# Attention's wide pairs with five PSUM banks, decay vectors in another place, sigmoids behind a copy, five raw weight slots

## The chip, the cores and the metric

One core of one Trainium2 chip runs the whole decoder layer. The metric is the device time of one execution in microseconds. TensorE multiplies (PE; PEld is its weight load), VectorE (DVE) and ScalarE (ACT) do the elementwise work, GpSimd (POOL) mostly issues transfers here, and SyncE (SP) issues the loads of weights. Each engine runs its own instructions strictly in order and waits on semaphores for the others.

## The reference, cut to what matters

```
f = swiglu(rms_norm(h, ffn1_norm_pre), ffn1_w_gate, ffn1_w_up, ffn1_w_down)
h = h + 0.5 * rms_norm(f, ffn1_norm_post)

u = rms_norm(h, mix_norm_pre)
q, k, v, xr, yr, gl = jnp.split(u @ w_in, splits, axis=-1)
# three groups of four heads, dilated windows, softmax over each window,
# the three groups merged by their log-sum-exp
attn_d = attn.reshape(B, S, ATTN_OUT_WIDTH) @ w_attn_branch

log_a = -LRU_C * gate_a * jax.nn.softplus(-a_param)
a = jnp.exp(log_a); b = jnp.sqrt(-jnp.expm1(2.0 * log_a)) * (gate_x * xc)
_, hs = lax.associative_scan(combine, (a, b), axis=1)
rec_d = (hs * jax.nn.gelu(yr)) @ w_rec_branch

gates = jax.nn.sigmoid(gl).reshape(B, S, N_BRANCHES, D_MODEL)
merged = gates[:, :, 0] * attn_d + gates[:, :, 1] * rec_d
h = h + rms_norm(merged @ w_out, mix_norm_post)
# and a second swiglu block of the form of the first
```

512 positions, 1024 wide, 12 heads of 128, feed-forward width 2816, all in float32. The only part of it that is not a matmul and that the change moves is `softplus(-a_param)`, 1024 values in all, and `sigmoid(gl)` for the first of the two branches.

## The kernel before, in words

**Numbers.** A float32 operand is held as two parts that TensorE takes at its fast rate: a high part, which is a copy by ACT (L302), and the rest, a subtraction by DVE (L303). Of each product of two operands three matmuls are done (high by high, high by low, low by high), at L315 to L317 for plain products. So each weight tile of 128x1024 that arrives as `raw` costs one ACT and one DVE instruction before TensorE can use it (`split`, L299 to L303).

**Weights.** One stream of weights, `in_w`, is read in a fixed order by SP (L242) into tiles `raw` of 128x1024 float32 that rotate through four slots; a load is issued when the slot's former tile has been read for the last time. The split tiles `w8` and `w4` have four and two slots of their own.

**Products by seven.** The large products are done in blocks of 2x2 with seven products in place of eight (p1 to p7); the sums of weight quarters that this needs are made by DVE (L691 to L696, L713; in the values stage L1221). The feed-forward blocks use `seven`'s narrow form for gate and up (L729 to L731) and `down7` for the way back (L1035 to L1037, which write banks `aux`; ACT seeds and empties these at L1024 and L1040).

**Wide pairs.** Queries, keys and the sigmoid inputs come from `seven_wide`: a product is four matmuls of 512 columns (L779: high weights by both parts of the activations) and four of 256 (L780: low weights by the high part) in turn, and its two outputs lie side by side in one bank. Seven products follow one another: p1, p5, p6, p2, p7, p3, p4. Between them a partial sum is kept in PSUM: `move` (L784) has ACT copy a whole bank into another, so that the next product accumulates on top of it; `fold` (L790, L791) has ACT copy one half out and DVE add the other; `sum_of` (L797, L798) has DVE add to sums that were folded out before. Four of the five `acc` banks serve a pair. The third move copies p7's sum into the bank of p1 and p2, `b`, once `fold(b, g[0])` has read it, since p4 has to accumulate on the copy.

**Order of the stages.** Feed-forward 1, the norms of boundary 1, the values (L1193 to L1195 `values_first`, L1236 to L1238 `values_two`), then for each of four heads three groups' queries and keys (`qk`, twelve wide pairs) with attention's own small work (`attend`) written between them: scores L1340 and L1341, exponentials L1359 and L1375, an exchange of maxima between partitions L1383 to L1389, transposes L1412, the weighted values L1430 and L1435. Then four wide pairs 52 to 59 whose outputs g and u go through a sigmoid (L1449, L1450), attention's output product, the recurrent part (LRU), its output product, boundary 2, and feed-forward 2. The decay vectors `po` and `sp8` (softplus of the recurrence's parameter, as a polynomial in 128x8 tiles) are made at the start of the LRU part (L1484 to L1500), 28 tiny DVE instructions and one exponential on ACT (L1486). They are first read as scales in the LRU's gates, at L1607.

**What sets the order.** A scheduler orders the instructions of each engine by the order of the source and by priorities: `high_priority(offset=...)` pulls its block forward (EVAC 200 for what empties banks, AHEAD 100 for weights), so that code of a later place in the source can come out among earlier code where its operands allow it. `issue_after(x)` only holds a block back until x has been placed. A function of ACT that is not in its loaded table needs a table load ahead of it (rows ACT_TABLE_LOAD).

**Space.** `npool` holds two 128x512 tiles, `acc` and `r`, for the norm at the start; `first_t` holds the first 512 columns of weights beside the small parameters `sm`. Both live for the whole kernel.

Of the kernel before, what the change touches and what calls it, by code (L numbers as in the profile page):

```python
# [10 lines left out]
F32 = mybir.dt.float32  # L11
F32R = mybir.dt.float32r
AF = mybir.ActivationFunctionType
ALU = mybir.AluOpType
AX = mybir.AxisListType

P = 128
T = 512
# [11 lines left out]
EPS = 1e-6  # L30
HB = 256
RAW_W = 1024
NEG = -1.0e30

FIRST_ON = {1: 5, 2: 5}
# [138 lines left out]
SMALL = {}  # L174
# [4 lines left out]
SMALL_W = _o  # L179
# [4 lines left out]
def hybrid_layer(ctx: ExitStack, tc: tile.TileContext, xT: bass.AP, xN: bass.AP, wst: bass.AP,  # L184
                 first: bass.AP, rows: bass.AP, consts: bass.AP, bias: bass.AP, out: bass.AP):
    nc = tc.nc
    DVE, ACT, PE = nc.vector, nc.scalar, nc.tensor

    cpool = ctx.enter_context(tc.tile_pool(name="cpool", bufs=1))
    bpool = ctx.enter_context(tc.tile_pool(name="bpool", bufs=6))  # L190
    wpool = ctx.enter_context(tc.tile_pool(name="wpool", bufs=4))
    tpool = ctx.enter_context(tc.tile_pool(name="tpool", bufs=4))
    npool = ctx.enter_context(tc.tile_pool(name="npool", bufs=1))
    psum = ctx.enter_context(tc.tile_pool(name="psum", bufs=1, space=bass.MemoryType.PSUM))
    dpool = ctx.enter_context(tc.tile_pool(name="dpool", bufs=1, space=bass.MemoryType.DRAM))

    first_t = cpool.tile([P, 512 + SMALL_W], F32, name="first")
    sm = first_t[:, 512:]
    cst = cpool.tile([P, CONST_W], F32, name="cst")
    ones = cpool.tile([P, P], F32, name="ones")  # L200
    eps = cpool.tile([P, 1], F32, name="eps")
    facc = cpool.tile([P, KC, T], F32, name="facc")
# [31 lines left out]
    def raw_of(key, dst=None):  # L234

        g, i = state["g"], state["i"]
        grp = groups[g]
        if i == 0:
            w = grp[-1][1] + grp[-1][2]
            raw = dst if dst is not None else wpool.tile([P, RAW_W], F32, name="raw", tag="raw", bufs=4)  # L240
            src = bass.AP(tensor=wst.tensor, offset=wst.offset + state["off"], ap=[[w, P], [1, w]])
            nc.sync.dma_start(raw[:, :w], src)  # L242
            state["raw"] = raw
            state["off"] += w * P
        k, o, w = grp[i]
        assert k == key, (k, key)
        src = state["raw"][:, o:o + w]
        if i + 1 == len(grp):
            state["g"], state["i"] = g + 1, 0
        else:  # L250
            state["i"] = i + 1
        return src
# [23 lines left out]

    def fetch_start():

        raws = [wpool.tile([P, RAW_W], F32, name="raw", tag="raw", bufs=4) for _ in range(4)]
        wts = []  # L280
        for k in range(KC):
            raw = raws[k // 2][:, (k % 2) * 512:(k % 2) * 512 + 512]
            if k == 0:
                raw = first_t[:, :512]
                nc.sync.dma_start(hm(k), xT[k])
                nc.sync.dma_start(raw, first[:, :512])
            else:
                nc.sync.dma_start(raw, bass.AP(tensor=wst.tensor, offset=wst.offset + (k - 1) * 512 * P,
                                               ap=[[512, P], [1, 512]]))
                nc.sync.dma_start(hm(k), xT[k])  # L290
            if k % 2 == 0:
                wt = w8()
            o = (k % 2) * 512
            wts.append((wt[:, 0, o:o + 512], wt[:, 1, o:o + 512], raw))
        state["g"], state["off"] = KC, (KC - 1) * 512 * P
        return wts
# [8 lines left out]
    def acc_ps():  # L305
        return psum.tile([P, T], F32, name="acc", tag="acc", bufs=5)
# [45 lines left out]
    HALVES = (slice(0, HB), slice(HB, T))  # L352
# [406 lines left out]
        seventh(t, w, "p4", v, False)  # L759
        u0(v)  # L760

    def seven_wide(t, w, g, u, seen=lambda ap: ap):


        b, v, z, y = (acc_ps() for _ in range(4))

        def two(ps):
            return ps[:, :HB], ps[:, HB:]

        def product(p, ps, start):  # L770
            at = t[p].at
            part, cross = ps.rearrange("q (s c) -> q s c", s=2), two(ps)[1]
            if len(at(0, 0).shape) == 3:
                part = ps.rearrange("q (s b t) -> q s b t", s=2, b=2)
                cross = cross.rearrange("q (b t) -> q b t", b=2)
            for k in range(4):
                ks = slice(k * P, (k + 1) * P)
                wh, wl = w[p][:, 0, ks], w[p][:, 1, ks]
                PE.matmul(part, wh, at(BOTH, k), start=start and k == 0, stop=False, skip_group_check=True)  # L779
                PE.matmul(cross, wl, at(0, k), start=False, stop=k == 3, skip_group_check=True)  # L780

        def move(dst, src):
            with tc.high_priority(offset=EVAC):
                ACT.activation(dst, src, AF.Copy)  # L784

        def fold(ps, dst=None):
            out = tpool.tile([P, HB], F32, name="c", tag="c", bufs=CB) if dst is None else dst
            x, y_ = two(ps) if dst is None else map(seen, two(ps))
            with tc.high_priority(offset=EVAC):
                ACT.activation(out, x, AF.Copy)  # L790
                DVE.tensor_add(out, y_, out)  # L791
            return out

        def sum_of(dst, ps, c):
            x, y_ = two(ps)
            with tc.high_priority(offset=EVAC):
                DVE.tensor_add(c, x, c)  # L797
                DVE.tensor_add(dst, seen(y_), seen(c))  # L798

        product("p1", b, True)  # L800
        move(y, b)
        product("p5", z, True)
        c5 = fold(z)
        product("p6", y, False)
        move(v, y)
        c6 = fold(y)
        product("p2", b, False)
        fold(b, g[0])
        product("p7", v, False)
        move(b, v)  # L810
        sum_of(u[1], v, c5)
        product("p3", z, False)
        sum_of(g[1], z, c6)
        product("p4", b, False)
        fold(b, u[0])

    def seven(t, w, z, g, u):

# [284 lines left out]
    ap1 = ff1.enter_context(tc.tile_pool(name="act1", bufs=1))  # L1103
    new_h()
    u1 = act_of(*act_two(ap1))
    acc = npool.tile([P, T], F32, name="acc", tag="acc", bufs=1)
    nc.scalar.dma_start(sm, first[:, 512:])
    warm(eps)

# [2 lines left out]
        PE.matmul(wu[:, :P], ones, ones, start=True, stop=True)  # L1112
    wts = fetch_start()
    pss = [acc_ps() for _ in range(4)]
    r1 = npool.tile([P, T], F32, name="r", tag="r", bufs=1)
    for k in range(KC):
        wh, wl, raw = wts[k]
        if k == 0:

            z = hm(0)  # L1120
            ACT.activation(u1.hi[0], z, AF.Copy, scale=col("g1a", 0))
            for sl in HALVES:
                tail = ACT.activation(wh[:, sl], raw[:, sl], AF.Copy).ins
            DVE.scalar_tensor_tensor(u1.lo[0], z, col("g1a", 0), u1.hi[0].bitcast(F32),
                                     op0=ALU.mult, op1=ALU.subtract)
# [35 lines left out]
    kpool = kpool_cm.__enter__()  # L1161

    def rec_half():

        return kpool.tile([P, 8, T], F32R, name="rb", tag="rb")

    with ExitStack() as mx:
        tpl = mx.enter_context(tc.tile_pool(name="attn_out", bufs=1))
# [37 lines left out]
        def values_two(steps, then):  # L1206
# [76 lines left out]
            for j in range(2):  # L1283
# [4 lines left out]
        t, steps = forms_of(lambda i, j: Form(lambda s, k: um_t[2 * i + k // 2][:, s, k % 2, HALVES[j]]),  # L1288
                            apool, False, rec_half)
# [12 lines left out]
        def pair_of(key):  # L1302

            i = order.index(key)
            if i + 1 < len(order):
                forms[order[i + 1]] = w_forms(order[i + 1])
            return forms.pop(key)
# [131 lines left out]

        for hd in range(NH):  # L1440
            attend(hd, qkvs.pop(hd))
            if hd + 1 < NH:
                qkvs[hd + 1] = qk(hd + 1)


        for c in range(0, KC, 2):
            g, u = tmp("g"), tmp("u")
            seven_wide(t, pair_of(("pair", 52 + c, 53 + c)), [g[:, h] for h in HALVES], [u[:, h] for h in HALVES])
            ACT.activation(facc[:, c, :], g, AF.Sigmoid)  # L1449
            ACT.activation(facc[:, c + 1, :], u, AF.Sigmoid, scale=-1.0)  # L1450
        apool_cm.__exit__(None, None, None)
        for c in range(KC):
            ps = acc_ps()
# [5 lines left out]
    with ExitStack() as mx:  # L1459
# [15 lines left out]
        lpool = lpool_cm.__enter__()  # L1475


        def s8(name):
            return lpool.tile([P, 8], F32, name=name)
        o, w = SMALL["ap"]  # L1480
        av = sm[:, o:o + w]
        na, ex, zz, po = (s8(n) for n in ("na", "ex", "zz", "po"))
        sp8 = s8("sp8")
        DVE.tensor_scalar(na, av, -1.0, None, op0=ALU.mult)  # L1484
        DVE.tensor_tensor(ex, av, na, op=ALU.min)
        ACT.activation(ex, ex, AF.Exp)  # L1486
        DVE.tensor_scalar(zz, ex, 2.0, None, op0=ALU.add)
        DVE.reciprocal(zz, zz)
        DVE.tensor_mul(zz, zz, ex)
        DVE.tensor_mul(ex, zz, zz)  # L1490
        DVE.memset(po, 1.0 / 19.0)
        for i in (17, 15, 13, 11, 9, 7, 5, 3, 1):
            DVE.tensor_mul(po, po, ex)
            DVE.tensor_scalar(po, po, 1.0 / i, None, op0=ALU.add)
        DVE.tensor_mul(po, po, zz)
        DVE.tensor_scalar(na, na, 0.0, None, op0=ALU.max)
        DVE.scalar_tensor_tensor(po, po, 2.0, na, op0=ALU.mult, op1=ALU.add)
        DVE.tensor_scalar(sp8, po, -8.0, None, op0=ALU.mult)
        sp4 = po
        DVE.tensor_scalar(sp4, po, 4.0, None, op0=ALU.mult)  # L1500

        def ip(ap):
            return ap.rearrange("q (i p) -> q p i", p=4)
# [124 lines left out]
        for i, (what, hd) in enumerate(LRU_ORDER):  # L1628
# [201 lines left out]
```

## Time and profile before

| | us |
|---|---|
| median of 3 runs | 1218.58 (1217.26 to 1219.91) |
| profiled execution | 1217.25 |
| its span | 1215.4 |
| PE busy | 1200.5 |
| DVE busy | 1030.6 |
| ACT busy | 835.9 |
| POOL busy | 26.2 |

The span is the time from the first to the last recorded instruction; some 1.9 us of the execution lie outside it. A busy time is a union of an engine's instructions. Matmuls overlap one another in the record (a 512-column matmul is drawn 0.39 us long and the next one starts 0.23 us after it), so a short stall shows as a later start rather than as an idle time. The granted TensorE clock is 0.999 over the execution. The stages lie about so: feed-forward 1 to 330 us, boundary 1 and values to 410, wide pairs with attention to 583, the sigmoid pairs to 607, attention's output and the LRU part to about 850, boundary 2 and feed-forward 2 from there to the end.

### The profile page before, as it was taken

To read this page: it belongs to the slowest core of one execution; us is meant where nothing else is said; L and a number is where in the kernel's file an instruction comes from. 1 tells how busy PE (TensorE), PEld (TensorE's weight loads), DVE (VectorE), ACT (ScalarE), POOL (GpSimd) and SP (SyncE) were. 2 spreads that over 40 slices of the span, in tenths; PEclk is the share of its full clock that TensorE was granted. 3 is DMA by queue.
4 is the path that set the end of the run, shared out by engine and by line. 5 is a ranking of instruction groups with operands and counts; after the bars stand their busy time and mean duration, and the time that the engine had idled before them with its cause. 6 is when DMAs were issued, how large, how long until landed. Compare 5 with 4: busy or idle time off the path is not lost.

```text
span 1215.4 us, 18988 instructions
## 1 busy us (share of the span) xinstructions
PE 1200.5 (99%) x7306; PEld 1073.9 (88%) x7306; DVE 1030.6 (85%) x1608; ACT 835.9 (69%) x1449; POOL 26.2 (2%) x51
## 2 busy tenths in 40 slices
PE   9999999999999999999999999999999999999997
PEld 8899999999887888888889888888899999999996
DVE  7999888989789899999867899875799888889964
ACT  7567787886575676777735898834566677877763
POOL 0000000001011000000000000000100000000000
PEclk9999999999999999999999999999999999999999
DMA  7234333434634232222323342235443343433341
GB/s 265 89 102 138 114 133 121 134 115 155 239 125 126 70 113 71 96 85 81 99 75 122 122 156 87 87 122 175 154 139 109 120 136 108 136 115 129 122 173 70
DMA packets 45818, 149.77 MB, mean 123 GB/s; under 512 B 5152, under 2 KB 8608, under 8 KB 45728
## 3 DMA queue, kind: packets, MB, share of 16 engines
q1 hardware_dynamic: 38160, 131.09, 32.5%
q0 software_dynamic: 7280, 17.30, 4.3%
q8 instruction: 57, 0.93, 0.3%
q14 instruction: 33, 0.27, 0.1%
q10 hardware_dynamic: 288, 0.17, 0.0%
HBM read 138.06 MB, written 6.29 MB: 119 GB/s over the span
## 4 chain that ended last, share of the span: by engine, by line
PE 89%; DVE 5%; ACT 3%; DMA 2%; issue 1%; SPq 0%; DVEq 0%; ACTq 0%
PE acc L729 10%; PE acc L731 10%; PE acc L730 10%; PE acc L315 7%; PE acc L317 7%; PE acc L316 7%; PE acc L779 7%; PE aux L1035 4%; PE aux L1036 4%; PE aux L1037 4%; PE acc L780 3%; DVE w L303 2%; PE acc L433 2%; PE acc L432 2%; PE acc L431 2%; DMA raw<-in_w 1%
## 5 line engine op out<-in xcount | busy, mean ns | idle before, releaser
L303 DVE TENSOR_TENSOR w<-raw,w 128x1024 fp32r<-128x1024 f32 (+1 forms) x272 | 297.5, 1098 | 36.2 <-ACT w L302 35.4
L302 ACT ACTIVATE w<-raw 128x1024 fp32r<-128x1024 f32 (+1 forms) x272 | 259.7, 959 | 92.1 <-PE acc L317 44.5
L729 PE MATMUL acc<-big,w 128*128 128x256 f32 x920 | 260.4, 283 | 0.0
L731 PE MATMUL acc<-big,w 128*128 128x256 f32 x920 | 260.3, 283 | 0.0
L730 PE MATMUL acc<-big,w 128*128 128x256 f32 x920 | 260.3, 283 | 0.0
L729 PEld LDWEIGHTS acc<-big,w 128*128 128x128 f32 x920 | 176.2, 192 | 1.9
L730 PEld LDWEIGHTS acc<-big,w 128*128 128x128 f32 x920 | 176.3, 192 | 1.7
L731 PEld LDWEIGHTS acc<-big,w 128*128 128x128 f32 x920 | 176.3, 192 | 0.0
L779 PE MATMUL acc<-big,w 128*128 128x512 f32 x320 | 115.2, 398 | 0.3 <-ACT acc L784 0.3
L780 PE MATMUL acc<-big,w 128*128 128x256 f32 x320 | 90.6, 283 | 0.0
L1035 PE MATMUL aux<-w,xf 128*128 128x512 f32 x224 | 87.5, 393 | 0.6 <-ACT w L302 0.6
L1036 PE MATMUL aux<-w,xf 128*128 128x512 f32 x224 | 87.5, 391 | 0.0
L1037 PE MATMUL aux<-w,xf 128*128 128x512 f32 x224 | 87.2, 389 | 0.0
L779 PEld LDWEIGHTS acc<-big,w 128*128 128x128 f32 x320 | 60.1, 188 | 13.7 <-ACT acc L784 0.6
L303 DVE TENSOR_TENSOR w<-s,w 128x1024 fp32r<-128x1024 f32 x51 | 62.2, 1220 | 4.9 <-ACT w L302 4.8
L780 PEld LDWEIGHTS acc<-big,w 128*128 128x128 f32 x320 | 60.5, 189 | 0.1
L315 PE MATMUL acc<-xf,w 128*128 128x512 f32 (+1 forms) x168 | 59.0, 353 | 0.0
L317 PE MATMUL acc<-xf,w 128*128 128x512 f32 (+1 forms) x168 | 58.5, 349 | 0.0
L316 PE MATMUL acc<-xf,w 128*128 128x512 f32 (+1 forms) x168 | 58.5, 349 | 0.0
L302 ACT ACTIVATE w<-s 128x1024 fp32r<-128x1024 f32 x51 | 53.8, 1056 | 6.2 <-PE acc L731 3.0
L743 ACT ACTIVATE c<-acc 128x256 f32<-128x256 f32 x74 | 28.2, 384 | 40.7 <-PE acc L731 40.7
L1035 PEld LDWEIGHTS aux<-w,xf 128*128 128x128 f32 x224 | 41.9, 188 | 9.3 <-ACT w L302 1.2
(454 smaller groups left out, 2938.6 us busy)
## 6 DMA issues: line engine op xcount, KB each, us to landing
raw<-in_w SPq DMA_DIRECT2D x232, 512.0 KB, 3.5
big<-xf POOLq DMA_DIRECT2D x6, 512.0 KB, 3.4
gains<-in_rows POOLq DMA_DIRECT2D x5, 512.0 KB, 5.7
h<-in_x SPq DMA_DIRECT2D x8, 256.0 KB, 5.3
h<-in_xn POOLq DMA_DIRECT2D x4, 512.0 KB, 6.7
kept_m<-h POOLq DMA_DIRECT2D x4, 512.0 KB, 2.9
vals<-in_w SPq DMA_DIRECT2D x4, 512.0 KB, 6.1
h<-kept_m POOLq DMA_DIRECT2D x4, 512.0 KB, 5.5
```

The costliest lines, as they stand in the source:

```text
L302: state["split"] = ACT.activation(dh, src, AF.Copy).ins
L303: DVE.tensor_sub(dl, src, dh.bitcast(F32))
L315: PE.matmul(ps, wh, xh, start=first, stop=False)
L316: PE.matmul(ps, wh, xl, start=False, stop=False)
L317: PE.matmul(ps, wl, xh, start=False, stop=last)
L729: PE.matmul(ps, wh, xh, start=start and k == 0, stop=False, skip_group_check=True)
L730: PE.matmul(ps, wh, xl, start=False, stop=False, skip_group_check=True)
L731: PE.matmul(ps, wl, xh, start=False, stop=k == 3, skip_group_check=True)
L779: PE.matmul(part, wh, at(BOTH, k), start=start and k == 0, stop=False, skip_group_check=True)
L780: PE.matmul(cross, wl, at(0, k), start=False, stop=k == 3, skip_group_check=True)
L1035: PE.matmul(ps, xh, wh, start=first and j == 0, stop=False, skip_group_check=True)
L1036: PE.matmul(ps, xh, wl, start=False, stop=False, skip_group_check=True)
```

## The change

```diff
+RAW_N = 5
...
-    npool = ctx.enter_context(tc.tile_pool(name="npool", bufs=1))
...
-    first_t = cpool.tile([P, 512 + SMALL_W], F32, name="first")
-    sm = first_t[:, 512:]
+    sm = cpool.tile([P, SMALL_W], F32, name="first")
...
-            raw = dst if dst is not None else wpool.tile([P, RAW_W], F32, name="raw", tag="raw", bufs=4)
+            raw = dst if dst is not None else wpool.tile([P, RAW_W], F32, name="raw", tag="raw", bufs=RAW_N)
...
-    def seven_wide(t, w, g, u, seen=lambda ap: ap):
+    def seven_wide(t, w, g, u, seen=lambda ap: ap, then=lambda: None):
-        b, v, z, y = (acc_ps() for _ in range(4))
+        b, z, y, v, o = (acc_ps() for _ in range(5))
...
         def move(dst, src):
             with tc.high_priority(offset=EVAC):
-                ACT.activation(dst, src, AF.Copy)
+                return ACT.activation(dst, src, AF.Copy).ins
...
         product("p7", v, False)
-        move(b, v)
+        moved = move(o, v)
         sum_of(u[1], v, c5)
+        with tc.issue_after(moved):
+            then()
         product("p3", z, False)
         sum_of(g[1], z, c6)
-        product("p4", b, False)
-        fold(b, u[0])
+        product("p4", o, False)
+        fold(o, u[0])
...
-    acc = npool.tile([P, T], F32, name="acc", tag="acc", bufs=1)
+    norm = ap1.tile([P, 2, T], F32, name="acc", tag="e", bufs=1)
+    acc, r1 = norm[:, 0], norm[:, 1]
...
+    def decay():
+        o, w = SMALL["ap"]
+        av = sm[:, o:o + w]
+        na, ex, zz = (s8(n) for n in ("na", "ex", "zz"))
+        po, sp8 = decays
+        DVE.tensor_scalar(na, av, -1.0, None, op0=ALU.mult)
+        DVE.tensor_tensor(ex, av, na, op=ALU.min)
+        ACT.activation(ex, ex, AF.Exp)
...
+        for i in (17, 15, 13, 11, 9, 7, 5, 3, 1):
+            DVE.tensor_mul(po, po, ex)
+            DVE.tensor_scalar(po, po, 1.0 / i, None, op0=ALU.add)
...
         for hd in range(NH):
             attend(hd, qkvs.pop(hd))
+            if hd == 1:
+                decay()
             if hd + 1 < NH:
                 qkvs[hd + 1] = qk(hd + 1)
...
+        two = []
+        def gate():
+            if two:
+                c, g, u = two.pop()
+                ACT.activation(facc[:, c, :], g, AF.Sigmoid)
+                ACT.activation(facc[:, c + 1, :], u, AF.Sigmoid, scale=-1.0)
         for c in range(0, KC, 2):
             g, u = tmp("g"), tmp("u")
-            seven_wide(t, pair_of(("pair", 52 + c, 53 + c)), [g[:, h] for h in HALVES], [u[:, h] for h in HALVES])
-            ACT.activation(facc[:, c, :], g, AF.Sigmoid)
-            ACT.activation(facc[:, c + 1, :], u, AF.Sigmoid, scale=-1.0)
+            seven_wide(t, pair_of(("pair", 52 + c, 53 + c)), [g[:, h] for h in HALVES], [u[:, h] for h in HALVES],
+                       then=gate)
+            two.append((c, g, u))
+        gate()
...
-        def s8(name):
-            return lpool.tile([P, 8], F32, name=name)
...
+        sp4, sp8 = decays
```

A pair takes all five `acc` banks, and p7's copy goes to a bank of its own, `o`. The sigmoids of a pair are issued behind the third move of the pair after it, those of the last pair behind the loop. The 28 instructions of the decay vectors are the same ones, written between the second head and the queries and keys of the third, in tiles that live to the end. Raw weights rotate through five slots; the space comes from `npool` and the first weight tile, which now use tiles that are free at that time (the pool of feed-forward 1 and `raws[0]`).

More of the change, by code (lines that the diff above doesn't have):

```diff
@@ L277, in fetch_start @@
     def fetch_start():
-        raws = [wpool.tile([P, RAW_W], F32, name="raw", tag="raw", bufs=4) for _ in range(4)]
+        raws = [wpool.tile([P, RAW_W], F32, name="raw", tag="raw", bufs=RAW_N) for _ in range(4)]
         wts = []
@@ L283, in fetch_start @@
             if k == 0:
-                raw = first_t[:, :512]
                 nc.sync.dma_start(hm(k), xT[k])
@@ L1114, in hybrid_layer @@
     pss = [acc_ps() for _ in range(4)]
-    r1 = npool.tile([P, T], F32, name="r", tag="r", bufs=1)
     for k in range(KC):
@@ L1165, in rec_half, with s8 @@
         return kpool.tile([P, 8, T], F32R, name="rb", tag="rb")
+    def s8(name):
+        return kpool.tile([P, 8], F32, name=name)
+    decays = [s8(n) for n in ("po", "sp8")]
+    def decay():
[6 more added lines that the diff above has]
+        ACT.activation(ex, ex, AF.Exp)
+        DVE.tensor_scalar(zz, ex, 2.0, None, op0=ALU.add)
+        DVE.reciprocal(zz, zz)
+        DVE.tensor_mul(zz, zz, ex)
+        DVE.tensor_mul(ex, zz, zz)
+        DVE.memset(po, 1.0 / 19.0)
+        for i in (17, 15, 13, 11, 9, 7, 5, 3, 1):
+            DVE.tensor_mul(po, po, ex)
+            DVE.tensor_scalar(po, po, 1.0 / i, None, op0=ALU.add)
+        DVE.tensor_mul(po, po, zz)
+        DVE.tensor_scalar(na, na, 0.0, None, op0=ALU.max)
+        DVE.scalar_tensor_tensor(po, po, 2.0, na, op0=ALU.mult, op1=ALU.add)
+        DVE.tensor_scalar(sp8, po, -8.0, None, op0=ALU.mult)
+        DVE.tensor_scalar(po, po, 4.0, None, op0=ALU.mult)
     with ExitStack() as mx:
@@ L1475, in hybrid_layer @@
         lpool = lpool_cm.__enter__()
-        def s8(name):
-            return lpool.tile([P, 8], F32, name=name)
[L1480 to L1500, printed above, removed]
+        sp4, sp8 = decays
         def ip(ap):
```

## The prediction

> **What bounds the kernel now.** I read the page first: the busy times and the chain that ended last.
>
> ```profile
> PE 1200.5 (99%) x7306; PEld 1073.9 (88%) x7306; DVE 1030.6 (85%) x1608; ACT 835.9 (69%) x1449; POOL 26.2 (2%) x51
> PE 89%; DVE 5%; ACT 3%; DMA 2%; issue 1%; SPq 0%; DVEq 0%; ACTq 0%
> ```
>
> TensorE is busy for 1200.5 of a span of 1215.4 us. The change removes no matmul, so all that it can win lies in the other 15 us, plus the slow restart after each stall. Next I asked who ends PE's waits (idle of PE itself, then of its weight load, where a short stall shows better), in the form "us in all, times, longest", and how full the engines are during attention.
>
> ```profile
> PE aux L315 <- ACT w L302: 1.5, 1, 1.5
> ...
> PE aux L1386 <- DVE xch L1383: 0.9, 1, 0.9
> ...
> PEld acc L779 <- ACT acc L784: 4.3, 8, 1.4
> PEld aux L1035 <- ACT w L302: 1.2, 3, 0.4
> PEld aux L1430 <- ACT facc L1415: 0.4, 1, 0.4
> ```
>
> ```profile
> 432.00:583.00 151.00, 149.91 (x926) 132.31 (x924) 143.61 (x311) 106.10 (x249) 0.00 (x0) 1.00 0.27 87
> ```
>
> The last row gives the stretch, its length, then the busy time of PE, PEld, DVE, ACT. The wide pairs' matmuls wait eight times, 4.3 us in all, for L784, the copy of a bank; it is the largest item that the change touches. PE idles 1.1 us in 151 there, and DVE only 7.4: work that comes to DVE in attention is not free.
>
> **Five banks.** A third copy before, in the chain of waits, and PE's pace around another one:
>
> ```profile
> 417.40 0.35 DVE qk L791
> ...
> 417.83 0.59 ACT acc L784
> ...
> 418.47 0.50 PE acc L779
> ```
>
> ```profile
> 478.00 0.28 PE L780 MATMUL acc<-big,w 128*128 128x256 f32 x1
> 478.27 0.50 PE L779 MATMUL acc<-rb,w 128*128 128x512 f32 x1
> 478.61 0.28 PE L780 MATMUL acc<-rb,w 128*128 128x256 f32 x1
> 478.73 0.40 PE L779 MATMUL acc<-rb,w 128*128 128x512 f32 x1
> ```
>
> The copy into `b` waits until DVE has read `b` (L791), and p4 waits for the copy. With bank `o` the copy needs p7's end alone, which lies a whole product (p3) ahead of p4. Of the eight waits three lie in the sigmoid pairs (2.5 of the 4.3 us, row below) and one of those, 0.4, is of this kind; with the five before it that is six waits and 4.3 − 2.5 + 0.4 = 2.2 us of weight-load idle. The matmuls lose less: at 478.27 the start comes 0.27 after the one before and the next 0.34 later, where 0.12 (478.61 to 478.73) and 0.23 are the pace, so some 0.26; I take 0.3 each, 1.8. In ACT's built order the copy comes behind the same weight copy as before, or earlier, so nothing new holds it. The first pair's 0.3 I do not count (DVE is late there, below). **−1.5**, bounds −1.0 and −2.2. The new cost: five tiles from five banks means that the next pair's p5 writes the bank from which DVE's `sum_of` read p3. Between lie p4 and the next p1, eight times 0.35 us; four additions at some 0.35 (the L791 row) end well before, so nothing.
>
> **Sigmoids behind a copy.** ACT's rows in the third sigmoid pair, and the waits in 583 to 608 us:
>
> ```profile
> 594.71 0.21 ACT L1486 ACTIVATE ex<-ex 128x8 f32<-128x8 f32 x1
> ...
> 597.05 1.28 ACT L1449 ACT_TABLE_LOAD   x1
> 598.35 0.63 ACT L1449 ACTIVATE facc<-g 128x512 f32<-128x512 f32 x1
> 598.88 0.58 ACT L784 ACTIVATE acc<-acc 128x512 f32<-128x512 f32 x1
> ```
>
> ```profile
> PEld acc L779 <- ACT acc L784: 2.5, 3, 1.4
> ```
>
> The bank copy at 598.88, on which the longest wait of 1.4 hangs, stands behind a table load (the decay's exponential had taken the sigmoid table out) and a sigmoid, 1.8 us of ACT. Both go from there: **−1.35**, bounds −1.0 and −1.4. Behind the next pair's third copy the sigmoids hold up only p3's later ACT work, due a product afterwards. The one table load left comes in the second pair, no longer ahead of the last head's transposes that ended the 0.4 at L1430: **−0.2**, bounds 0 and −0.4.
>
> **A fifth raw slot.** One wait on PE goes back to a raw load:
>
> ```profile
> 598.29 0.03 DVE po L1494
> 598.32 3.41 DMA raw<-in_w
> ...
> 602.93 0.50 PE acc L779
> ```
>
> That load left only when DVE had freed a slot. With five, every load on SP's queue waits for the tile one further back, so this one is there in time: **−0.6** (the third of the three waits, 2.5 − 1.4 − 0.4), bounds 0 and −0.7. In SP's order one raw load comes ahead of the values' four loads, but it waits only for a tile that DVE frees before boundary 1's end, earlier than what held the values' loads: no delay.
>
> **The exchange.** In the built order three more couples of wide matmuls (3 × 0.35 us) stand before the exchange matmul L1386, and one more addition on DVE (0.35) before its operand. Of the 0.9: **−0.7**, bounds 0 and −1.
>
> **The recurrent part.** Its one stall, the 1.5 at L315, ends with a weight copy of ACT that stands behind a chain of DVE's work in the built order. About one DVE instruction of that chain now comes later. **−0.5**, bounds 0 and the whole stall, −1.6.
>
> **The decay vectors, where they land.** The priorities carry them forward. In the built order nine of the DVE instructions and the exponential come in boundary 1, some 358 to 364 us, eighteen among the last values and the first wide pair, 400 to 418, two later.
>
> ```profile
> L1493 DVE TENSOR_TENSOR po<-po,ex x9: 166/168/169, 596.9 to 601.3; 128x8 f32<-128x8 f32 x9
> ```
>
> ```profile
> 366.27 1.23 DVE L1221 TENSOR_TENSOR vals<-vals 128x1024 f32<-128x1024 f32 x1 [1.10 <-DMA vals<-in_w]
> ...
> 382.17 2.35 DVE L303 TENSOR_TENSOR w<-vals,w 128x1024 fp32r<-128x1024 f32 x2
> 384.44 2.36 DVE L1221 TENSOR_TENSOR vals<-vals,raw 128x1024 f32<-128x1024 f32 x2
> ...
> 409.36 1.23 DVE L303 TENSOR_TENSOR w<-raw,w 128x1024 fp32r<-128x1024 f32 x1 [1.28 <-ACT w L302]
> ```
>
> ```profile
> 383.44 0.50 PE L1237 MATMUL aux<-w,rb 128*128 128x512 f32 x1 [1.32 <-DVE w L303]
> ```
>
> At 0.168 us and a little between, one takes 0.2. In boundary 1 the table load and the exponential (1.28 + 0.21) stand ahead of ACT's copies of the normed input, and DVE's work behind them slips by as much; but one DVE instruction of 1.13 us (2.27 for two, 382.17 to 384.44) has moved behind the values' first weights, and DVE waits 1.10 us for the load that lands at 366.27. So that load still comes last. From there to the release of 383.44 the new order counts fifteen such instructions, as the old: no change. Behind it one has moved ahead of an operand that PE needs 23 matmuls later: 383.4 + 5 × 1.13 = 389.1 against 383.44 + 23 × 0.23 = 388.7, **+0.45** with the restart. The eighteen, 3.6 us, meet 1.28 us of idle DVE at 409.36; the remaining 2.3 stretches DVE through the first pair, where p4 no longer waits for it and the first scores do: **+0.2**. Together **+0.65**, bounds −0.5 and +2.7 (0.45 and all 2.3).
>
> The Trainium skill, "ScalarE: Activation LUTs", section "What ACT_TABLE_LOAD costs", puts a switch at 1283 ns for the load plus some 1380 ns of drain. The trace agrees with the first (1.28) and shows nothing of the second: the sigmoid starts 1.30 us after the load at 597.05. By the page ACT would be another 1.4 us late in boundary 1, more than what the values' load hides, and the sum some 0.7 us higher.
>
> **Feed-forward 1.** The order shows a side effect. In feed-forward 2 a group of `down7` matmuls comes three times right behind a single product, and waits:
>
> ```profile
> 1020.78 0.95 ACT w L302
> ...
> 1021.78 0.73 PE aux L1035 x2
> ```
>
> The weight copy stands behind the eviction of the group before it: 0.4 us of weight load each (the 1.2, 3 above) and 0.07 of restart. The new order has three such places in feed-forward 1, which had none, and one fewer in feed-forward 2: 3 × 0.47 − 0.47 = **+0.95**, bounds −0.5 and +1.4.
>
> **Sum.** −1.5 − 1.35 − 0.2 − 0.6 − 0.7 − 0.5 + 0.65 + 0.95 = −3.25 us. From the profiled execution's 1217.25 that is 1214.0; the median of the runs lies 1.33 above that execution: **1215.3**. Less than 0.2%, 2.4 us, can't be told from no change by a measurement of this kernel.
>
> **Rivals.**
>
> *DVE takes it back.* If DVE is attention's true limit, a wait that leaves the bank returns at the next weight tile or the scores. For it: its 143.61 of 151 us, and DVE ahead of the copy in the chain at 417.40. Against it: PE idles so little there that DVE can't have been late often. Then the five banks and the exchange give nothing: −3.25 + 2.2 = −1.05, 1217.5. Chance 0.26.
>
> *The decay vectors land on the path, and it is slower.* From 366.27 on PE waits for DVE, and it is there that the order puts most of them. If all 27 delay DVE's weight tiles one for one, and the idle at 409.36 is no cover since the copy that DVE waits for there slips too, 27 × 0.2 + 1.5 + 0.45 = 7.35 us arrive in place of 0.65: 1215.3 + 6.7 = 1222.0. It decides from 5.7 us over my sum. Against it: nine run where DVE waits for a load, and five banks give PE's copies room. Chance 0.14.
>
> *The change doesn't do what it says.* The vectors aren't between heads at all: that is in the sum. A fifth slot without effect, since loads are 2% of the chain, costs its 0.6: 1215.9, within the forecast.
>
> **How the numbers follow.** Forecast 0.60, DVE takes it back 0.26, slower 0.14. All terms at their better bound give −8.3 (1210.3), all at the worse −1.0 − 1.0 + 2.7 + 1.4 = +2.1 (1220.7); both ends together are unlikely, so the range is 1210.5 to 1220. The forecast's own range is 1212.5 to 1216.5. 0.2% begins at 1216.1: of the forecast 0.02 lie within it, and 0.01 of the first rival beyond the other side: faster 0.58, within 0.2% 0.27, slower 0.15.
>
> **What would show it.** Right: no L779 waits for L784 behind L791; the waits at 599 and 602 are gone; one sigmoid table load in place of two; three new waits of L1035 for L302 before 330 us; L1237 near 383 still waits for DVE as long. Wrong: L1237 near 383 or the first scores (L1340) more than a microsecond later, new waits of L779 for weight tiles from DVE in the heads, or waits of L1035 in feed-forward 1 of more than half a microsecond each.

## The result, and the profile after

The changed kernel is slower: median 1223.08 us (1221.02 to 1225.06, 6 runs) against 1218.50 (1217.26 to 1219.91) for the kernel before, ratio 1.0036 with a 95% interval of 1.0023 to 1.0049. The forecast was 1215.3, range 1210.5 to 1220; the sign was wrong. Its profiled execution took 1221.02 us, span 1219.2, 3.8 us above the span before.

The page of the changed kernel, span and busy times:

```profile
span 1219.2 us, 18968 instructions
...
PE 1203.2 (99%) x7306; PEld 1073.5 (88%) x7306; DVE 1029.5 (84%) x1608; ACT 834.2 (68%) x1447; POOL 26.1 (2%) x51
```

The same 7306 matmuls keep PE busy for 2.7 us more (1200.5 before), and PE idles 16.0 us instead of 14.9. So most of the loss isn't idle time at all: matmuls start later or run slower while PE counts as busy. Who ended PE's idle time, in the form of the prediction (us in all, times, longest), first in the kernel before, as far as not shown yet, then in the changed one (L1263 to L1265 are the lines L1236 to L1238 of before, L300 and L301 are L302 and L303, L313 to L315 are L315 to L317, L727 to L729 are L729 to L731, L741 is L743, L777 and L782 are L779 and L784, L1248 is L1221; L1035 is L1035):

```profile
PE aux L1237 <- DVE w L303: 2.5, 2, 1.3
...
PE acc L779 <- ACT acc L784: 1.4, 2, 1.1
...
PE aux L1035 <- ACT w L302: 0.6, 3, 0.2
```

```profile
PE aux L1264 <- DVE w L301: 3.6, 3, 1.6
PE aux L1035 <- ACT w L300: 1.2, 5, 0.4
PE aux L314 <- DVE rec L301: 1.1, 1, 1.1
PE aux L313 <- ACT w L300: 1.1, 2, 0.8
...
PE acc L727 <- ACT c L741: 0.7, 2, 0.4
PE acc L727 <- ACT acc L741: 0.6, 2, 0.4
```

What the change aimed at is gone from the list: the 1.4 us of bank copies and the 0.9 of the exchange, 2.3 together. In its place stand 1.1 more in the values (L1264, 3.6 against 2.5), 0.6 more at L1035 (five waits against three), 0.7 more at the recurrent part's weights (1.1 + 1.1 against 1.5) and 1.3 at products by seven (L727, one wait in the recurrent part and three in feed-forward 2) that waited for nobody before: 3.7.

And the matmuls themselves. Two stretches of the kernel before, then of the changed one: attention's output product, and the recurrent part's (in brackets after PE's busy time, the matmuls):

```profile
607.00:627.00 20.00, 20.00 (x92) 16.61 (x91) 14.51 (x22) 6.19 (x8) 0.00 (x0) 1.00 0.30 101
783.00:823.00 40.00, 40.00 (x178) 33.15 (x177) 31.04 (x40) 16.97 (x22) 0.00 (x0) 1.00 0.33 108
```

```profile
607.00:627.00 20.00, 20.00 (x87) 16.10 (x86) 13.99 (x20) 5.79 (x8) 0.00 (x0) 1.00 0.30 100
783.00:823.00 40.00, 40.00 (x174) 32.42 (x173) 31.07 (x41) 17.98 (x24) 0.00 (x0) 1.00 0.32 111
```

PE is never idle there and its granted clock reads 1.00 in all four rows, yet it does 174 matmuls in 40 us where it did 178. (In the first pair the stretch holds a few shorter wide-pair matmuls too, so the second is the clean one: 2% slower.)

Two theories followed, with the letters that the expectations below use. F, the fifth raw slot: the new waits in feed-forward 1, the recurrent part and feed-forward 2. D, the decay vectors: their order in the values, and (A) the addresses of what is laid out behind them. In the built program the five tiles of 32 bytes push `attn`, `vals`, `rec`, `sig` and `qk` to addresses 32 above a multiple of 64; before, all of these and `rb` began at multiples of 256. The rival to A was O: the slow matmuls are chance, or come with the order.

### The profile page after: what moved, and what is told of

It reads as the page before. It is cut to its first block, busy times and chain, and to the rows that moved or that the text cites. A ratio compares the mean times of both kernels' runs of the same rounds, so it can differ in the third digit from the quotient of the medians.

```text
span 1219.2 us, 18968 instructions
## 1 busy us (share of the span) xinstructions
PE 1203.2 (99%) x7306; PEld 1073.5 (88%) x7306; DVE 1029.5 (84%) x1608; ACT 834.2 (68%) x1447; POOL 26.1 (2%) x51
## 4 chain that ended last, share of the span: by engine, by line
PE 82%; DVE 8%; ACT 6%; DMA 3%; issue 1%; SPq 0%; DVEq 0%; ACTq 0%
PE acc L727 8%; PE acc L729 8%; PE acc L728 8%; PE acc L777 8%; PE acc L315 7%; PE acc L313 7%; PE acc L314 7%; PE acc L778 4%; DVE w L301 3%; PE aux L1035 3%; PE aux L1036 3%; PE aux L1037 3%; ACT w L300 2%; PE acc L430 2%; PE acc L431 2%; PE acc L429 2%
## 5 line engine op out<-in xcount | busy, mean ns | idle before, releaser
L301 DVE TENSOR_TENSOR w<-raw,w 128x1024 fp32r<-128x1024 f32 (+1 forms) x272 | 297.1, 1097 | 55.7 <-ACT w L300 55.0
L300 ACT ACTIVATE w<-raw 128x1024 fp32r<-128x1024 f32 (+1 forms) x272 | 260.0, 958 | 91.2 <-PE acc L315 43.3
L727 PE MATMUL acc<-big,w 128*128 128x256 f32 x920 | 260.4, 283 | 0.7 <-ACT c L741 0.7
L729 PE MATMUL acc<-big,w 128*128 128x256 f32 x920 | 260.3, 283 | 0.0
L727 PEld LDWEIGHTS acc<-big,w 128*128 128x128 f32 x920 | 176.2, 192 | 2.9 <-ACT c L741 1.1
L729 PEld LDWEIGHTS acc<-big,w 128*128 128x128 f32 x920 | 176.2, 192 | 0.0
L777 PE MATMUL acc<-big,w 128*128 128x512 f32 x320 | 115.1, 399 | 0.0
L1035 PE MATMUL aux<-w,xf 128*128 128x512 f32 x224 | 87.3, 393 | 1.2 <-ACT w L300 1.2
L777 PEld LDWEIGHTS acc<-big,w 128*128 128x128 f32 x320 | 60.1, 188 | 13.4
L301 DVE TENSOR_TENSOR w<-s,w 128x1024 fp32r<-128x1024 f32 x51 | 62.1, 1217 | 2.3 <-ACT w L300 1.8
L313 PE MATMUL acc<-xf,w 128*128 128x512 f32 (+1 forms) x168 | 58.8, 352 | 0.0
L315 PE MATMUL acc<-xf,w 128*128 128x512 f32 (+1 forms) x168 | 58.6, 349 | 0.0
L314 PE MATMUL acc<-xf,w 128*128 128x512 f32 (+1 forms) x168 | 58.6, 349 | 0.0
L300 ACT ACTIVATE w<-s 128x1024 fp32r<-128x1024 f32 x51 | 53.8, 1055 | 5.0 <-PE acc L729 2.4
L741 ACT ACTIVATE c<-acc 128x256 f32<-128x256 f32 x74 | 28.3, 383 | 40.8 <-PE acc L729 40.6
L1035 PEld LDWEIGHTS aux<-w,xf 128*128 128x128 f32 x224 | 41.8, 188 | 10.1 <-ACT w L300 2.2
```

The lines of the kernel that those rows point to most:

```text
L300: state["split"] = ACT.activation(dh, src, AF.Copy).ins
L301: DVE.tensor_sub(dl, src, dh.bitcast(F32))
L313: PE.matmul(ps, wh, xh, start=first, stop=False)
L314: PE.matmul(ps, wh, xl, start=False, stop=False)
L315: PE.matmul(ps, wl, xh, start=False, stop=last)
L727: PE.matmul(ps, wh, xh, start=start and k == 0, stop=False, skip_group_check=True)
```

## Experiments

Each was compared with runs of the kernel before on its chip; twelve kernels in three groups.

### Tiles of 64 bytes

```diff
-        return kpool.tile([P, 8], F32, name=name)
+        return kpool.tile([P, 16], F32, name=name)[:, :8]
```

> The changed kernel with its five small decay tiles 64 bytes long in place of 32 (16 floats, 8 of them used), so that the tiles laid out behind them start at multiples of 64 bytes again, as in the kernel before. Nothing else moves; the order on each engine stays that of the changed kernel. Theory A (addresses: the matmuls of attention's output product and of the recurrent output run 2 to 3% slower in the changed kernel because attn and rec lie 32 bytes off a multiple of 64): the 512-column matmuls at 606 to 630 us and at 782 to 830 us start each 0.227 us again instead of 0.232, and the time falls by 1.5 to 2.6 us, to about 1221. Theory O (order alone: the slower matmuls are chance or a throttle): no difference within 0.7 us, 1223.

Ratio 1.0038 (1.0025 to 1.0051): no gain. Neither theory is served by the time alone; the rows divide it.

```profile
607.00:627.00 20.00, 20.00 (x91) 16.51 (x90) 14.74 (x22) 6.60 (x10) 0.00 (x0) 1.00 0.31 106
783.00:823.00 40.00, 40.00 (x175) 32.55 (x174) 31.10 (x41) 18.37 (x25) 0.00 (x0) 1.00 0.37 119
```

Attention's output product is back at nearly its pace, the recurrent product is not. With this padding `attn` and `rec` begin 64, `rb` 128 above a multiple of 256. PE's busy time, 1205.0, can't be compared here: in this trace TensorE runs from 375.26 to 378.68 us at a granted clock of 0.50 (more on such stretches under e4). A, as I had put it (multiples of 64 are enough), is wrong; whether any alignment is the cause was open until the next runs.

### Four raw slots

```diff
-RAW_N = 5
+RAW_N = 4
```

> The changed kernel with four raw slots in place of five, all else as changed. Theory F (the fifth slot is what costs: it brings the three waits of L1035 in feed-forward 1 and the new waits at 1041, 1045, 1085 and 1105 us in feed-forward 2, and gives 0.6 at 602): the built order has no group of two down matmuls in feed-forward 1, so 3 x 0.47 us go there and 1 to 2 us in feed-forward 2, 0.5 comes back there (the third such place) and 0.6 in the sigmoid pairs: 1.5 to 2.5 us faster than the changed kernel, 1220.6 to 1221.6. Theory D (the decay vectors and their addresses are what costs): 1223 to 1224.

Ratio 1.0003 (0.9994 to 1.0012), against 1.0036: 0.33%, 4.0 us, went with the slot, more than expected. Who ended PE's idle time here:

```profile
PE aux L1264 <- DVE w L301: 3.6, 3, 1.9
PE aux L313 <- ACT w L300: 1.5, 1, 1.5
PE aux L1113 <- DVE eps L227: 1.1, 1, 1.1
PE aux L1035 <- ACT w L300: 0.6, 3, 0.2
```

All waits of L727 are gone, L313's is the single 1.5 of the kernel before, L1035 waits three times again; the values' 3.6 stays. So F holds for the two feed-forward blocks and the recurrent part, and not for the values.

### Decay vectors late, and then a shift of 32 bytes put back

The changed kernel with the decay vectors made at the start of the recurrent part, as before (e3); then the same with one small tile more (e4).

```diff
-            if hd == 1:
-                decay()
...
+        DVE.memset(kpool.tile([P, 8], F32, name="gap"), 0.0)
         qkvs = {0: qk(0)}
```

> The changed kernel with the decay vectors made at the start of the recurrent part as before, in tiles of that part; five banks, sigmoids behind a copy and five raw slots stay. Theory D (the decay vectors cost by their order in the values and by the addresses of their tiles): the values lose only the 2.8 us that they lost before (1.3 and 1.5 at L1237) instead of 5, and the matmuls are at their old pace: 4 to 5 us faster than the changed kernel, 1218 to 1219. Theory F (the fifth slot): 1 us faster at most, 1222.

> The kernel of e3_late with one more tile of 32 bytes in the pool that lives to the end (written once by a small memset), so that attn, rec, vals, qk and sig lie 32 bytes off a multiple of 64 again while the decay vectors stay late. Theory A (addresses): 1.5 to 2.6 us slower than e3_late, with the slower matmuls at 606 to 630 and 782 to 830 us back. Theory O: the same as e3_late within 0.7 us.

e3: ratio 1.0014 (1.0005 to 1.0023); e4: 1.0029 (1.0018 to 1.0041). The first lies 0.22%, 2.7 us, below the changed kernel, between theory D's 4 to 5 and theory F's 1 at most. Part of the shortfall is in its trace: with the vectors late, a wait of 0.7 us at 598 for a bank copy (L782) is back. The second lies 0.15%, 1.8 us, above the first, inside what A asked for; the two intervals overlap a little. PE's busy time and the recurrent product, e3 and then e4:

```profile
PE 1201.3 (99%) x7306; PEld 1074.8 (88%) x7306; DVE 1028.7 (84%) x1608; ACT 834.8 (69%) x1449; POOL 26.1 (2%) x51
...
783.00:823.00 40.00, 40.00 (x178) 33.15 (x177) 30.37 (x39) 16.31 (x21) 0.00 (x0) 1.00 0.34 117
```

```profile
PE 1204.4 (99%) x7306; PEld 1076.1 (88%) x7306; DVE 1029.2 (84%) x1609; ACT 834.7 (68%) x1449; POOL 26.1 (2%) x51
...
783.00:823.00 40.00, 40.00 (x175) 32.40 (x174) 30.84 (x41) 17.78 (x24) 0.00 (x0) 1.00 0.34 112
```

A tile that holds nothing of use, and PE is busy 3.1 us longer with the same matmuls in the same order. Not all of it is the address. In e4 a stretch of 3.41 us, right behind two waits of PE, has half the granted clock:

```profile
691.32:694.73 3.41, 3.41 (x19) 3.41 (x18) 3.41 (x6) 0.89 (x3) 0.63 (x2) 0.50 0.47 147
```

Comparing the start of each matmul in e4 with the start of the same one in e3, 1.5 of the 3.1 us arise there. The stretch from 783 to 823 us has a clock of 1.00 in both, and its 175 against 178 remain. Against O, chance, stand these rows, those of e6 below, and the pair of e2 and e11 further down.

### Tiles of 256 bytes

```diff
-        return kpool.tile([P, 8], F32, name=name)
+        return kpool.tile([P, 64], F32, name=name)[:, :8]
```

> The changed kernel with each small decay tile 256 bytes long, so that all tiles behind them start at multiples of 256 as in the kernel before. After e1_pad64, theory A reads: a multiple of 64 is not enough (in e1_pad64 rec at 64 and rb at 128 above a multiple of 256 still took 0.230 to 0.234 us for a 512-column matmul). Theory A: 0.227 in attention's output product and in 782 to 830 us, and 1.5 to 2.5 us less than the changed kernel, 1220.5 to 1221.5. Theory O: as e1_pad64, 1222.

Ratio 1.0022 (1.0012 to 1.0033), median 1220.75, as A expected, 0.14% or 1.7 us below the changed kernel, though the intervals overlap. The rows are plain:

```profile
PE 1200.7 (99%) x7306; PEld 1073.7 (88%) x7306; DVE 1029.6 (85%) x1608; ACT 834.4 (69%) x1447; POOL 26.1 (2%) x51
...
783.00:823.00 40.00, 40.00 (x178) 33.15 (x177) 31.27 (x40) 17.21 (x22) 0.00 (x0) 1.00 0.32 110
```

178 matmuls again, and PE busy 2.5 us less than in the changed kernel, in the same order of instructions; neither trace holds a stretch at half the clock between its start and its end.

### Five banks and sigmoids, without slot and decay

Both together (e5), then each alone in the kernel before (e9, e10).

```diff
-        b, v, z, y = (acc_ps() for _ in range(4))
+        b, z, y, v, o = (acc_ps() for _ in range(5))
...
-        move(b, v)
+        moved = move(o, v)
...
+        with tc.issue_after(moved):
+            then()
```

> Five banks and the sigmoids behind a copy alone: four raw slots, the decay vectors late as in the kernel before, and so no shifted tiles. If the cost lies wholly in the fifth slot (order in both feed-forward blocks and the recurrent part) and in the decay vectors (values, addresses), this keeps what attention and the sigmoid pairs gained in the changed kernel (7.5 us of stalls before in 400 to 606 us, 3.3 less in e3_late) and nothing else: 2.5 to 3.5 us faster than the kernel before, ratio 0.997 to 0.998. Rival, DVE takes it back: within 0.7 us of the kernel before.

> The kernel before with five banks in the wide pairs and nothing else. Prediction's term: six waits of L779 for L784 go (6 x 0.3 us) and part of the exchange (0.7): 1.5 to 2.5 us faster than before, ratio 0.998 to 0.9988. Rival, DVE takes it back: within 0.7 us. If the exchange follows the fifth bank wholly, up to 3 us.

> The kernel before with the sigmoids of a pair behind the third copy of the next pair, four banks, decay vectors late. e5_banks_gate kept a stall of 0.9 us at 597, since the late exponential still takes the sigmoid table out, so of the 1.35 predicted only some 0.5 and of the 602 wait up to 0.6 should go: 0.5 to 1.5 us faster than before, ratio 0.9988 to 0.9996. With e9_banks it should add up to e5_banks_gate (0.996). Rival: most of e5's gain is the sigmoids' and not the banks': 0.9975.

e5: 0.9960 (0.9948 to 0.9972), 4.9 us, more than expected. e9, the banks: 0.9967 (0.9955 to 0.9980). e10, the sigmoids: 0.9999 (0.9990 to 1.0008). The new places of the norm's tiles and of the first weights are in all three, so e10 shows that they cost nothing by themselves. The banks give 4.0 us, more than I expected, and the rival "DVE takes it back" falls: no entry in the list of PE's waits lies between 410 and 583 us in e9. The sigmoids alone give nothing, where I expected 0.5 to 1.5 us. ACT in e5, and PE's row there:

```profile
594.78 1.28 ACT L1495 ACT_TABLE_LOAD   x1
596.07 0.21 ACT L1495 ACTIVATE ex<-ex 128x8 f32<-128x8 f32 x1
596.19 0.58 ACT L782 ACTIVATE acc<-acc 128x512 f32<-128x512 f32 x1
```

```profile
596.82 0.50 PE L777 MATMUL acc<-rb,w 128*128 128x512 f32 x1 [0.72 <-ACT acc L782]
```

The sigmoids are out of the copy's way, but the late exponential takes its place with its own table load, 1.28 us. In e10, with four banks, a second wait is new besides: 1.08 us at 606.61, for a bank copy that itself waits for DVE. That moving the sigmoids pays where the exponential is gone as well is what the traces suggest (e7 below has no such wait, and its matmuls gain 2.3 us on those of e5 between 583 and 607); by time e7 lies only 0.09% below e5, inside the intervals.

### The fifth slot alone

The kernel before with five raw slots and the space made for them.

```diff
-... tag="raw", bufs=4)
+... tag="raw", bufs=RAW_N)
```

> The kernel before with five raw slots (and the space for them from the norm's tiles and the first weights' tile) and nothing else. Theory F: the three new waits in feed-forward 1 (+1.4), the waits in the recurrent part (+1.1) and in feed-forward 2 (+1.5 to 2.8), less 0.6 in the sigmoid pairs: 3 to 4.5 us slower than before, ratio 1.0025 to 1.0037. If the fifth slot costs only together with the other parts: 1.5 us slower at most.

Ratio 1.0039 (1.0025 to 1.0053): by itself it costs 4.8 us, a little more than expected and as much as the whole change. How it costs, in two places of the changed kernel. In feed-forward 1 (the chain of waits):

```profile
106.06 1.06 ACT w L300
107.12 0.04 issue
107.17 0.73 PE aux L1035 x2
```

And in the recurrent part, ACT's rows before, then after:

```profile
640.10 1.28 ACT L1565 ACT_TABLE_LOAD   x1
641.39 0.63 ACT L1565 ACTIVATE ge<-ge 128x512 f32<-128x512 f32 x1
641.93 0.37 ACT L743 ACTIVATE acc<-acc 128x256 f32<-128x256 f32 x1
642.23 0.61 ACT L302 ACTIVATE w<-raw 128x512 fp32r<-128x512 f32 x1
```

```profile
639.51 0.63 ACT L300 ACTIVATE w<-raw 128x512 fp32r<-128x512 f32 x1
640.15 1.28 ACT L1581 ACT_TABLE_LOAD   x1
641.45 0.63 ACT L1581 ACTIVATE ge<-ge 128x512 f32<-128x512 f32 x1
641.99 0.37 ACT L741 ACTIVATE acc<-acc 128x256 f32<-128x256 f32 x1
```

```profile
642.41 0.38 PE L727 MATMUL acc<-rb,w 128*128 128x256 f32 x1 [0.39 <-ACT acc L741]
```

The weight copy has moved from behind the bank copy (L741, L743 before) to ahead of the table load: its 0.63 us now come before something for which PE waits. As I read the order, a load that can land earlier lets the scheduler place the copy of that weight earlier, and on an engine that runs in order earlier for a weight is later for a bank. The same slot taken from the changed kernel (e2) shows where the time goes. Both have 7306 matmuls, so the start of the n-th can be compared: the changed kernel falls 1.4 us behind e2 in feed-forward 1 and 1.7 between 640 and 700 us, gains 0.5 between 900 and 1000, and loses 1.4 between 1000 and 1100.

### Decay vectors held, free, and held with five slots

The changed kernel with four slots and 256-byte tiles, and the vectors held until the second head's last instruction has been placed (e7); without the hold (e11); e7 with five slots (e12).

```diff
-            attend(hd, qkvs.pop(hd))
+            done = attend(hd, qkvs.pop(hd))
             if hd == 1:
-                decay()
+                with tc.issue_after(done):
+                    decay()
```

> The changed kernel with four raw slots, decay tiles of 256 bytes, and the decay vectors held back until the last instruction of the second head has been placed, so that they really come between heads. Theory D (in the values the vectors' order cost 2 us, their addresses 1.5 to 2.5): as e5_banks_gate less the exponential's table loads late in the sigmoid pairs (0.9 at 597 us in e3_late), more what 28 small instructions cost DVE in the third head, some 0 to 1 us: 1213.5 to 1215.5 beside 1217.8 before, the fastest of all. Rival: DVE, 95% busy in attention, passes on their 5.6 us: 1217 to 1219.

> e7_held4 without the hold: four raw slots, five banks, sigmoids behind a copy, decay tiles of 256 bytes, and the scheduler free to pull the decay vectors into boundary 1 and the values. What is left between the two is the order alone. Theory D: the values' stalls at L1264 (0.36, 2.0 and 1.7 us in e2_raw4, 1.1 and 1.5 in e7_held4) and 0.3 later: 1.5 to 2.5 us slower than e7_held4, ratio 0.9963 to 0.9972. Rival, the addresses were all of it: 0.995.

> e7_held4 with five raw slots: the change as its words have it, all decay vectors between heads and no tile moved off its multiple of 256. Theory F: the fifth slot costs what it cost alone (e8_raw5only, 0.39%): 4 to 5 us slower than e7_held4, ratio 0.9985 to 0.9995, and the waits in feed-forward 1, the recurrent part and feed-forward 2 back in the trace. Rival: it cost only beside the old attention: within 1.5 us of e7_held4.

e7: 1212.55 us, ratio 0.9951 (0.9938 to 0.9964), the fastest of all by median (its interval overlaps those of e5 and e9) and faster than both kernels; I had expected 1213.5 to 1215.5. e11: 0.9978 (0.9968 to 0.9989), 0.27% or 3.3 us slower than e7 with no other edit than the hold, more than the 1.5 to 2.5 expected. e12: 0.9992 (0.9984 to 1.0001), 0.41% or 5.0 us above e7 by the slot alone. DVE in the values, the changed kernel and then e7:

```profile
367.79 1.23 DVE L1248 TENSOR_TENSOR vals<-vals 128x1024 f32<-128x1024 f32 x1 [1.59 <-DMA vals<-in_w]
368.93 1.22 DVE L301 TENSOR_TENSOR w<-raw,w 128x1024 fp32r<-128x1024 f32 x1
371.03 1.23 DVE L1248 TENSOR_TENSOR vals<-vals 128x1024 f32<-128x1024 f32 x1 [0.88 <-DMA vals<-in_w]
372.17 3.49 DVE L301 TENSOR_TENSOR w<-raw,w 128x1024 fp32r<-128x1024 f32 x3
```

```profile
365.82 1.23 DVE L1248 TENSOR_TENSOR vals<-vals 128x1024 f32<-128x1024 f32 x1 [0.87 <-DMA vals<-in_w]
366.96 1.22 DVE L301 TENSOR_TENSOR rb<-ts,rb 128x1024 fp32r<-128x1024 f32 x1
368.10 4.63 DVE L301 TENSOR_TENSOR w<-raw,w 128x1024 fp32r<-128x1024 f32 x4
372.64 1.22 DVE L1248 TENSOR_TENSOR vals<-vals 128x1024 f32<-128x1024 f32 x1
```

The small instructions themselves are not what is late. With them the scheduler put the second half of the values' sum ahead of three of the first four weights, and that half's load lands only at 371.03. In e7 the four weights run through while it lands, and 372.64 waits for nothing. e11 has the changed kernel's order here, and the second wait with it:

```profile
369.52 1.23 DVE L1248 TENSOR_TENSOR vals<-vals 128x1024 f32<-128x1024 f32 x1 [1.13 <-DMA vals<-in_w]
```

PE's stall at L1264 follows in the changed kernel:

```profile
373.44 0.50 PE L1264 MATMUL aux<-w,big 128*128 128x512 f32 x1 [1.58 <-DVE w L301]
```

In the traces PE is 2.7 us further behind in e11 than in e7 when the values end at 410. That isn't the wait alone: right behind a wait of 1.8 us at L1264 stands again a stretch of 3.41 us at a clock of 0.50 (373.26 to 376.67). Half of it, 1.7 us, is my estimate of its price. The changed kernel's trace has no such stretch there, and PE loses 2.2 us on the kernel before in the values.

**The addresses once more.** e11 and e2 differ in the padding of the decay tiles alone, and every engine has the same order of instructions in both. Their ratios, 0.9978 and 1.0003, lie 0.25% or 3.0 us apart, and the intervals don't meet. The recurrent product in e2, then in e11:

```profile
783.00:823.00 40.00, 40.00 (x174) 32.48 (x173) 29.91 (x38) 15.74 (x20) 0.00 (x0) 1.00 0.34 108
```

```profile
783.00:823.00 40.00, 40.00 (x178) 33.12 (x177) 29.80 (x38) 15.70 (x21) 0.00 (x0) 1.00 0.35 116
```

This is the clearest pair for theory A, though the two ran on different chips, each against the kernel before on its own.

## Why the prediction was wrong

The forecast was −3.25 us, and +4.4 was measured (0.36%). Removing one part after another gives each part's share (the changed kernel, e2, e5, e9, before; the lines of the prediction in brackets):

| part | predicted | measured |
|---|---|---|
| banks (−1.5, exchange −0.7) | −2.2 | −4.0 |
| sigmoids (−1.35, −0.2) | −1.55 | −0.9, inside the intervals |
| decay vectors (+0.65) | +0.65 | +5.3 |
| fifth slot (−0.6, recurrent part −0.5, feed-forward 1 +0.95) | −0.15 | +4.0 |

Two steps failed, the slot by 4.2 us and the decay vectors by 4.7.

*Five banks, −1.5, and the exchange, −0.7.* Right in mechanism and too small: −4.0 us alone (e9; the interval spans 2.4 to 5.5). I left out the first pair: of the 3.1 us that e9's matmuls gain on the kernel before between 410 and 583 us, 0.8 lie there (410 to 432). The rival that I gave 0.26, DVE taking it back, is refuted.

*Sigmoids, −1.35 and −0.2.* The waits at 599 and 602 are gone from the changed kernel, and its matmuls gain 2.5 us on the kernel before between 583 and 607. But I booked this to the wrong edit: the sigmoids alone give nothing (e10), and the traces put most of it down to the exponential's departure (e7 against e5), which no time here resolves.

*A fifth raw slot, −0.6.* This step failed, and with it the sign. The wait at 602 did go, but it is gone with four slots as well (e2), so nothing of the −0.6 is the slot's. Instead the slot costs 4.8 us by itself (0.39%, e8) and 4.0 to 5.0 in company (e2, e12). The feed-forward 1 places that I had read off the built order came as priced: three new waits of L1035, the first at 107 us, 1.4 us. What I did not do was price the rest of the same reordering. For feed-forward 2 I took one place less, −0.47; that came, but three waits of L727 came with it, 1.4 us. For the recurrent part I wrote −0.5 with no bound on the side of a loss, from one instruction that came later, without following PE's next waits (L727 for a bank copy, L314 for DVE, 1.1); it lost 1.7.

*Decay vectors, +0.65.* Two parts of this step failed. The count of fifteen instructions to the release at 383 was right, but "the load still comes last" took the four loads of the values for one: DVE needs two halves, the new order asks for the second half earlier, and its landing time couldn't be read before because DVE reached it late. The order is 3.3 us (e11 against e7; the bound was 2.7). The second wait for the load is 1.1 of it; the stretch at half the clock behind PE's stall and the sum at L667, which now stands behind the values' first weights, were not separated from it. And I gave the tiles no price for their place in memory: 1.7 to 3.0 us (e6, e4, and e2 against e11), a term that was not in the sum at all. Less 1.1 us for the exponential's departure (e7 against e5, inside the intervals), 3.3 and 3.0 make up the 5.3 but for rounding.

*The rival "slower", 0.14, 1222.0.* Near in time and wrong in mechanism: no one-for-one delay by small instructions; the price came from the slot, a reordered load and addresses.

*The page on table loads.* By the Trainium skill's "ScalarE: Activation LUTs", section "What ACT_TABLE_LOAD costs", a drain of 1.4 us would have followed the load in boundary 1. The changed kernel shows none:

```profile
360.73 1.28 ACT L1179 ACT_TABLE_LOAD   x1
362.02 0.21 ACT L1179 ACTIVATE ex<-ex 128x8 f32<-128x8 f32 x1
```

The next row starts 1.29 us after the load's start, as at 597 before (1.30). The 0.7 us of that sentence did not arise.

Three things stay open. Why the scheduler regroups just these places when a slot is added was seen in its order only, not tried. How an address slows a matmul is not known. And the runs of some kernels scatter more (1217.62 to 1224.86 in e6, 1212.20 to 1213.34 in e7). The granted clock goes with it in part: the changed kernel took 1221.02 to 1223.08 us in its three runs at 0.999 and 1223.08 to 1225.06 in the three at 0.997, and all five runs of e7 are at 0.999. The stretches at half the clock in four of the traces (e1, e4, e11, e12) each come within 1.5 us behind a wait of PE of 1.1 to 2.1 us. But the changed kernel has such waits without one, so what brings them was not found, and a share of the times above may be theirs.

## What to carry to other kernels

Another buffer isn't free where a scheduler orders by when data can be there: compare the whole new order, not only the place that the buffer is for, and price every bank copy that a weight copy has passed. Before moving work into a stage, ask when each load of that stage lands by itself; a wait that isn't in the trace may only be covered by the order. And place small tiles behind the large ones or pad them, and compare the number of matmuls in a stretch without waits, after a look at its granted clock.

## What the runs showed of the hardware

The place of tiles in memory changes the pace of matmuls with no idle time and a granted clock that reads 1.00: 174 and 175 in 40 us where the large tiles begin 32 bytes above a multiple of 64 (changed kernel, e2, e4), 175 at 64 and 128 above a multiple of 256 (e1), 178 or 179 in the ten kernels where they begin at multiples of 256. By the mean distance of starts in the traces, 512 columns of `rec` take some 234 ns at 32 above a multiple of 64 (changed kernel, e4), 230 at 64 above one of 256 (e1) and 227 at a multiple of 256. The tile's own address isn't all: `rb` takes 229 ns in e4, where it begins at a multiple of 256 itself and the tiles beside it don't. Which multiple is the least that suffices, and for which of the operands, was not tried.

Four traces hold one stretch of 3.41 or 3.42 us at a granted clock of 0.50 inside the kernel, and TensorE does 256 columns in 0.21 us there instead of 0.12 (e4, 691 to 695 us). PE counts as busy all the time.
